# Turning the residual's blocks as fp32r in the last stage of a two-layer decoder trunk, with four blocks turned both ways

## The chip, the core and the metric

The kernel runs on one core of a Trainium2 chip. The metric is device time in microseconds, the median of several runs of the whole program; lower is better. A core has a matrix engine (PE, with its weight loads shown apart as PEld), a vector engine (DVE), a scalar engine (ACT), a general engine (POOL) and a queue that issues transfers (SP). Matrix products are written to PSUM, from which DVE and ACT read them; everything else lies in SBUF, and inputs and outputs in device memory.

## What is computed

Two pre-norm residual layers over a sequence of 1024 positions with 1024 features, and a last RMS norm. Layer 0 mixes with a gated linear recurrence, layer 1 with forgetting attention (16 heads of 64). The part that matters here is the end of layer 1 and the last norm:

```python
def fox_mixer(h, w_in, b_f, w_out):
    ...
    o = jnp.transpose(o, (1, 0, 2, 3, 4)).reshape(bsz, s, FOX_WIDTH).astype(h.dtype)
    y = o * jax.nn.silu(gate)
    return y @ w_out.astype(h.dtype)

def reference(x, ...):
    for i in range(DEPTH):
        h = rms_norm(x, norm_g[i])
        ...
            x = x + fox_mixer(h, fox_w_in[j], fox_b_f[j], fox_w_out[j])
    return rms_norm(x, final_g)
```

## The kernel before

The kernel keeps activations transposed: features on the 128 partitions, positions along the free axis, in two halves `c` of 512 positions. Products with 512 columns run in fp32r, a float32 that the matrix engine takes in one go at less precision; to keep precision, each operand is split into a high and a low part (`to_hi`, `to_lo`), and three products (high by high, high by low, low by high) are summed in PSUM. Blocks that are turned (`transpose`, or `matmul` with `is_transpose=True`) use the f32 identity `ident`, made at the start by POOL.

Layer 1 walks over the 16 heads. For each head and half, `maxima` computes scores and exponentials, and `weigh` turns these blocks (tile `pt`), splits them and multiplies them with the values (tile `O`). Between its steps `run` takes steps from a generator `fill`, which holds other work for PE; `side` holds more of it. In the last heads the fill is: the last projections, then `partial`, which adds six of the eight pairs of heads of the output projection to the residual and writes it back to the scratch tensor `x1d`, and then `turned`, the last stage. A scheduler of the framework, not the source alone, puts the instructions of each engine into their final order; within an engine the order is then fixed, and the engines wait for each other by semaphores.

`turned(c, q)` finishes a quarter of 256 positions. `residual` loads the residual so far from `x1d`, as eight blocks of 128 features by 256 positions. For each block `b` of 128 positions it goes over the features in parts (normally two of 512, in the very last block 512, 256 and 256). For each part it takes one PSUM buffer (tile `turn`), turns four (or two) residual blocks into it with the identity (line 921), and adds to it six products of the last two pairs of heads with the output weights. I call this one *group*: four turns and six products for 512 features. The stage has 17 groups: eight for c = 0 (two quarters, two blocks, two parts) and nine for c = 1.

A group is taken out of PSUM in two steps. ACT squares it with a running sum (`sq`, line 931), and DVE then multiplies it by the final norm's weights into `res` (line 933, or 939 for the last part of a block). DVE's step follows ACT's, and only then is the buffer free. The PSUM tag "g" has two buffers, as has "O"; groups use "g", apart from the first two groups of the second block of each quarter with c = 1, which use "O". The squares go to an SBUF scratch with the tag "xp", which has two buffers too.

For c = 0 the rows of the output wait for the whole half: `finish` (a `side` of the last run) takes one root for all four blocks (`root_mean`, lines 953 to 956, on the sums `ssq`), scales the four `res` (line 1058) and stores them (line 1059). For c = 1 each block has its own root, is scaled half by ACT (line 941) and half by DVE (line 942), and is stored (line 944). While c = 0 runs, the last head's work (`pt`, `O`) stands between and inside the groups on PE; the c = 1 part is PE groups alone.

Of the kernel before, what the change touches and what calls it, by code (L numbers as in the profile page):

```python
# [11 lines left out]
F32 = mybir.dt.float32  # L12
F32R = mybir.dt.float32r
BF16 = mybir.dt.bfloat16
AF = mybir.ActivationFunctionType
ALU = mybir.AluOpType

P = 128
SEQ = 1024
HALF = 512  # L20
# [18 lines left out]
def trunk(ctx: ExitStack, tc: tile.TileContext, xt, w0, wg, wo0, pc, gn, gf, w1, wv, wf, bf, wo1, out):  # L39
    nc = tc.nc  # L40

    def pool(name, bufs, **kw):
        return tc.tile_pool(name=name, bufs=bufs, **kw)

    const = ctx.enter_context(pool("const", 1))
# [3 lines left out]
    ps = ctx.enter_context(pool("ps", 2, space=PSUM))  # L49
# [3 lines left out]
    def matmul(*args, **kw):  # L53
        pe[0] = nc.tensor.matmul(*args, **kw)  # L54
        return pe[0]
# [5 lines left out]

    ident = const.tile([P, P], F32, name="ident")
    make_identity(nc, ident)
    onesf = const.tile([P, P], F32, name="onesf")
    nc.vector.memset(onesf, 1.0)
    epst = const.tile([P, 1], F32, name="epst")
# [116 lines left out]
    with ExitStack() as l0:  # L183
# [40 lines left out]
        xs = [[xpool.tile([P, HALF], F32, name=f"x{h}{k}") for k in range(KT)] for h in range(2)]  # L224
# [234 lines left out]
        for h, cs in enumerate(halves):  # L459
# [4 lines left out]
            for d0 in range(0, KT, 4):  # L464
                pts = []
                for db in range(d0, d0 + 4):
                    if db % 2 == 0:
                        two = ps.tile([P, 2, HALF], F32, tag="S", name="ops")
                    pts.append(two[:, db % 2])
                    mm3(pts[-1], wl[db][0], y[0], True, False)  # L470
                for db, o in enumerate(pts, d0):
                    mm3(o, wl[db][1], y[1], False, True)
                    x = xs[h][db]
# [18 lines left out]
    with ExitStack() as l1:  # L492
        tu = l1.enter_context(pool("tu", 1))
        at = l1.enter_context(pool("at", 2))
# [390 lines left out]
        def residual(c, q):  # L885

            cs = slice(q * 256, (q + 1) * 256)
            if c == q == 0:
                xs = [vpool.tile([P, 256], F32, tag=f"v{d}", name="x1", bufs=2) for d in range(KT)]
                for d, x in enumerate(xs):  # L890
                    nc.sync.dma_start(x, x1d[c, :, d, cs])
                return xs
            xs = [wpool.tile([P, 2, 256], F32, tag=("wl", "wh")[q], name="x1") for d in range(4)]
            for d, x in enumerate(xs):
                nc.sync.dma_start(x, x1d[c, :, 2 * d : 2 * d + 2, cs])
            return [x[:, i] for x in xs for i in range(2)]

        def turned(c, q):


            xs = left.pop((c, q), None) or residual(c, q)

            if c == 0:
                res = tu.tile([P, 2, SEQ], F32, tag=f"T{q}", name="res")
                res = [res[:, b] for b in range(2)]
            elif q == 0:
                res = [tu.tile([P, SEQ], F32, tag=t, name="res") for t in ("U", "U0")]
            else:
                res = [tu.tile([P, SEQ], F32, tag="U1", name="res"), at.tile([P, SEQ], F32, tag="p7", name="res", bufs=1)]
            for b in range(2):  # L910
                cs = slice(q * 256 + b * P, q * 256 + (b + 1) * P)

                parts = ((0, 4), (4, 2), (6, 2)) if c * q * b else ((0, 4), (4, 4))
                ss = ssq[c][:, 4 * q + 2 * b :][:, : len(parts)]
                for h, (d0, nd) in enumerate(parts):
                    hs = slice(d0 * P, (d0 + nd) * P)
                    pt = ps.tile([P, HALF], F32, tag="gO"[c * b] if h < 2 else "g", name="turn")[:, : nd * P]

                    for i in range(nd):
                        x = xs[d0 + i][:, b * P : (b + 1) * P]  # L920
                        matmul(pt[:, i * P : (i + 1) * P], x, ident, start=i == 0, stop=False, is_transpose=True)
                    for k in range(2):
                        yh, yl = (z[:, cs] for z in y1[c][6 + k])
                        wh, wl = (z[:, k::2][:, d0 % 4 : d0 % 4 + nd] for z in late_w[d0 // 4])
                        matmul(pt, yh, wh, start=False, stop=False)
                        matmul(pt, yl, wh, start=False, stop=False)
                        matmul(pt, yh, wl, start=False, stop=k == 1)
                        if k == 0:
                            yield
                    sq = at.tile([P, HALF], F32, tag="xp", name="sq1", bufs=2)[:, : nd * P]  # L930
                    nc.scalar.activation(sq, pt, AF.Square, accum_out=ss[:, min(h, ss.shape[1] - 1)].unsqueeze(1))
                    if c == 0 or h < len(parts) - 1:
                        nc.vector.tensor_tensor(res[b][:, hs], pt, grow[:, hs], ALU.mult)
                        if h == 1 and c == 1:
                            nc.vector.tensor_tensor(ss[:, 0:1], ss[:, 0:1], ss[:, 1:2], ALU.add)
                            ss = ss[:, 0::2]
                        yield
                if c == 1:
                    r = root_mean(ss, lambda: nc.vector.tensor_tensor(res[b][:, hs], pt, grow[:, hs], ALU.mult))
                    lo, hi = halves  # L940
                    nc.scalar.activation(res[b][:, lo], res[b][:, lo], AF.Copy, scale=r)
                    nc.vector.tensor_scalar(res[b][:, hi], res[b][:, hi], r, None, ALU.mult)
                    for hs in halves:
                        nc.sync.dma_start(out[4 + 2 * q + b, :, hs], res[b][:, hs])
                    yield
            if c == 0:
                first_half.extend(res)

        def root_mean(ss, between=lambda: None):

            ss = ss.rearrange("p (b h) -> p b h", h=2)
            r = ss[:, :, 0]
            nc.vector.tensor_tensor(r, r, ss[:, :, 1], ALU.add)
            between()
            nc.scalar.activation(r, r, AF.Sqrt, bias=epst, scale=1.0 / SEQ)
            nc.vector.reciprocal(r, r)
            return r
# [33 lines left out]
        for hd in range(HEADS):  # L991
            pair = hd // 2
            if hd % 2 == 0:
                if hd < 12:
                    fill = kq_units(pair + 1, ((1, (0, 1)), (0, (0,))))
                elif hd == 12:
                    pairs = ((0, 1), (2, 3), (4, 5), (6, 7))
                    todo = [(db, c) for two in pairs for c in range(2) for db in two]
                    splits = [split_loaded(c) for c in range(2)]
                    fill = chain(  # L1000
                        kq_units(7),
                        g_units(7, (0,)),
                        load_y(0),
                        first_out(),
                        beside(g_units(7, (1,)), 2, splits[0]),
                        load_y(1),
                        beside(beside(partial(todo), 0, splits[0]), 4, splits[1]),
                        turned(0, 0),
                        turned(0, 1),
                    )  # L1010
            elif pair < 6:
                fill = chain(kq_units(pair + 1, ((0, (1,)),)), late_q(hd + 1), g_units(pair + 1))
# [40 lines left out]
        def finish():  # L1053
# [3 lines left out]
            for i, o in enumerate(first_half):  # L1057
# [3 lines left out]
                yield  # L1061

        run("." * 20, fill=chain(turned(1, 0), turned(1, 1)), side=finish())


# [36 lines left out]
def build(arrays):  # L1102
    import concourse.bacc as bacc

    nc = bacc.Bacc("TRN2", target_bir_lowering=False, num_devices=1)
    args = [
        nc.dram_tensor(f"in_{k}", v.shape, mybir.dt.from_np(v.dtype), kind="ExternalInput").ap()
        for k, v in arrays.items()
    ]
    args.append(nc.dram_tensor("out_t", (KT, P, SEQ), F32, kind="ExternalOutput").ap())  # L1110
    with tile.TileContext(nc, schedule_with_timeline_sim=True) as tc:
        trunk(tc, *args)
    return nc
# [9 lines left out]
```

## Time and profile before

| what | value |
|---|---|
| median of 3 runs | 1123.81 us (1123.08 to 1123.89) |
| profiled execution, its span | 1127.7 us |
| PE busy, share of the span | 99% |
| PEld, DVE, ACT, POOL busy | 83%, 67%, 52%, 17% |
| groups of the last stage on PE | from about 1087.9 us to 1121.4 us |
| from the last product to the end of the span | 6.3 us |
| mean granted clock of PE | 0.998 |

The durations below come from one profiled execution; its span is longer than the time of the runs shown. A row of a timeline gives the start in us, the duration in us, the engine, the line and operation, what it writes and reads, the shape and how many instructions are merged into it, and in brackets how long the engine sat idle before and what released it. The start of a matmul is shown with its weight load (PEld) ahead of it; matmuls overlap, so the step of PE is read from start to start, not from the durations. A row of a group of instructions ends with busy time in us, mean duration in ns, and idle time before.

### The profile page before, as it was taken

The page shows a single profiled execution, that of the slowest core. Times are in us where ns is not written, and L with a number is a line of the kernel's source. Part 1 is how long each engine was busy: PE and PEld are TensorE (multiplying, and loading weights), DVE is VectorE, ACT ScalarE, POOL GpSimd, SP SyncE. Part 2 cuts the span into 40 slices and gives each one's busy share as a digit, 9 for nine tenths or more (in the row PEclk, how much of TensorE's full clock was granted, in tenths as well). Part 3 has the DMA queues.
Part 4 walks back from the last instruction along what each step waited for, and adds up shares of the span by engine and source line. Part 5 has one row for each costly group of instructions (what it writes and reads, how often), then busy time and mean ns, then how long its engine had stood idle before and what let it go on. Part 6 is the DMA issues. An engine that isn't in the chain of part 4 may idle for free.

```text
span 1127.7 us, 15774 instructions
## 1 busy us (share of the span) xinstructions
PE 1114.3 (99%) x5691; PEld 936.8 (83%) x5691; DVE 758.6 (67%) x1268; ACT 589.3 (52%) x1081; POOL 195.6 (17%) x155
## 2 busy tenths in 40 slices
PE   9999999999999999999999999999999999999997
PEld 7788888888888887988888988889888898888786
DVE  7888755776568789656676466664667646676545
ACT  8488345355453656365555355553555535644335
POOL 1322112221121201431021110212102110021220
PEclk9999999999999999999999999999999999999999
DMA  6111111111111114433425224242252422564345
GB/s 235 57 47 42 51 52 52 38 58 45 52 38 52 47 44 145 129 112 102 112 71 123 66 77 117 72 118 71 74 119 73 118 71 77 176 189 158 117 154 187
DMA packets 62902, 105.43 MB, mean 93 GB/s; under 512 B 9796, under 2 KB 24772, under 8 KB 62824
## 3 DMA queue, kind: packets, MB, share of 16 engines
q1 hardware_dynamic: 59704, 95.97, 28.9%
q0 software_dynamic: 3120, 8.46, 2.3%
q8 instruction: 45, 0.74, 0.3%
q14 instruction: 33, 0.27, 0.1%
HBM read 63.30 MB, written 15.93 MB: 70 GB/s over the span
## 4 chain that ended last, share of the span: by engine, by line
PE 92%; DMA 2%; DVE 2%; issue 1%; ACT 1%; SPq 1%; POOL 0%; DVEq 0%; POOLq 0%; ACTq 0%
PE gps L54 33%; PE ops L54 16%; PE ups L54 12%; PE vps L54 8%; PE S L54 6%; PE O L54 6%; PE pt L58 5%; PE gate L54 3%; PE turn L54 3%; DMA wf<-in_wo 1%; DMA x<-in_xt 1%; POOL wl L96 0%; PE rsrow L54 0%; DMA wf<-in_w 0%; DMA yhl<-y1d 0%
## 5 line engine op out<-in xcount | busy, mean ns | idle before, releaser
L54 PE MATMUL gps<-hh,wh 128*128 128x512 f32 x576 | 229.1, 398 | 0.6 <-DVE qkl L595 0.6
L54 PE MATMUL gps<-hh,wl 128*128 128x512 f32 x576 | 226.8, 394 | 0.0
L54 PE MATMUL gps<-hl,wh 128*128 128x512 f32 x576 | 226.7, 394 | 0.0
L85 ACT CAST wh<-wf 128x512 fp32r<-128x512 f32 (+2 forms) x156 | 94.2, 607 | 147.8 <-PE ops L54 55.3
L96 POOL TENSOR_TENSOR wl<-wf,wh 128x512 fp32r<-128x512 f32 (+1 forms) x60 | 101.0, 1689 | 389.8 <-ACT wh L85 362.5
L720 ACT ACTIVATE p<-S,m 128x128 f32<-128x128 f32 (+7 forms) x128 | 94.8, 741 | 137.9 <-DVE m L715 136.8
L96 DVE TENSOR_TENSOR pl<-pt,ph 128x512 fp32r<-128x512 f32 (+1 forms) x198 | 98.7, 540 | 88.1 <-ACT ph L85 87.6
L54 PEld LDWEIGHTS gps<-hl,wh 128*128 128x128 f32 x576 | 108.3, 188 | 24.7 <-issue 0.5
L54 PEld LDWEIGHTS gps<-hh,wh 128*128 128x128 f32 x576 | 108.6, 189 | 20.5 <-DVE qkl L595 0.8
L54 PEld LDWEIGHTS gps<-hh,wl 128*128 128x128 f32 x576 | 108.7, 189 | 20.1 <-POOL wl L96 0.6
L715 DVE CUSTOM_DVE_ANT_0 S<-S,mask 128x128 f32<-128x128 f32 (+7 forms) x128 | 97.3, 761 | 28.8 <-PE S L54 28.8
L85 ACT CAST ph<-pt 128x512 fp32r<-128x512 f32 (+1 forms) x198 | 83.6, 473 | 36.2 <-PE pt L58 28.9
L54 PE MATMUL S<-T,U 96*128 96x512 f32 (+7 forms) x384 | 91.9, 348 | 2.7 <-ACT p L720 2.7
L96 DVE TENSOR_TENSOR wl<-wf,wh 128x512 fp32r<-128x512 f32 x96 | 70.7, 741 | 28.3 <-ACT wh L85 27.4
L381 DVE TENSOR_TENSOR x<-x,ops 128x512 f32<-128x512 f32 x80 | 54.1, 683 | 48.0 <-PE ops L54 48.0
L54 PEld LDWEIGHTS S<-T,U 128*128 128x128 f32 (+1 forms) x384 | 68.6, 190 | 16.1 <-ACT p L720 3.5
L58 PE MATMUL pt<-ident,p 128*128 128x128 f32 x576 | 79.4, 273 | 0.8 <-DVE pl L96 0.5
L58 PEld LDWEIGHTS pt<-ident,p 128*128 128x128 f32 x576 | 67.2, 140 | 13.9 <-issue 2.9
L54 PE MATMUL ups<-hh,wh 128*128 128x512 f32 x192 | 76.1, 397 | 1.1 <-ACT hh L87 1.1
L54 PE MATMUL ups<-hl,wh 128*128 128x512 f32 x192 | 76.7, 399 | 0.2
L54 PE MATMUL ops<-yh,wh 128*128 128x512 f32 x192 | 76.0, 396 | 0.5 <-DVE x L474 0.5
L54 PE MATMUL ups<-hh,wl 128*128 128x512 f32 x192 | 76.2, 397 | 0.0
(183 smaller groups left out, 2247.8 us busy)
## 6 DMA issues: line engine op xcount, KB each, us to landing
wf<-in_w SPq DMA_DIRECT2D x100, 256.0 KB
wf<-in_wo SPq DMA_DIRECT2D x64, 128.0 KB
U<-qkh SPq DMA_DIRECT2D x64, 128.0 KB
T<-qkh SPq DMA_DIRECT2D x28, 256.0 KB
x<-in_xt SPq DMA_DIRECT2D x16, 256.0 KB
x1d<-x SPq DMA_DIRECT2D x16, 256.0 KB
wf<-in_wv SPq DMA_DIRECT2D x16, 256.0 KB
U<-qkl SPq DMA_DIRECT2D x32, 128.0 KB
```

The lines of the kernel that those rows point to most:

```text
L54: pe[0] = nc.tensor.matmul(*args, **kw)
L58: pe[0] = nc.tensor.transpose(*args)
L85: nc.scalar.copy(hi, src)
L96: return eng.tensor_tensor(lo, src, f32(hi), ALU.subtract)
L381: nc.vector.tensor_tensor(x, x, pt, ALU.add)
L715: nc.vector.tensor_tensor_reduce(S[:, :n], S[:, :n], mask[:, SEQ - n :], -1.0, -NEG, ALU.add, ALU.min, accum_out=m)
L720: seen[0] = nc.scalar.activation(p, S[:, :n], AF.Exp, bias=m, scale=-1.0, accum_out=sums[:, i : i + 1])
```

## The change

An fp32r copy of the identity is made once by ACT. The turns of the residual's blocks in the last stage take the residual and the identity as fp32r (the residual's bits as they are), and write PSUM as fp32r. For c = 0, after a quarter's groups, the first block of each `b` is turned twice into the two halves of a new PSUM tile `two` of the tag "g": once as fp32r, once as f32 as before. ACT copies the first result into `one` (scratch tag "xp"), DVE subtracts the second, and DVE adds 1e6 times the difference to the first 128 columns of `res`. So the output is changed wherever the two ways of turning differ. That makes four such pairs, and a step of the generator after each.

```diff
     ident = const.tile([P, P], F32, name="ident")
     make_identity(nc, ident)
+    identr = const.tile([P, P], F32R, name="identr")
+    nc.scalar.copy(identr, ident)
...
                     for i in range(nd):
                         x = xs[d0 + i][:, b * P : (b + 1) * P]
-                        matmul(pt[:, i * P : (i + 1) * P], x, ident, start=i == 0, stop=False, is_transpose=True)
+                        o = pt[:, i * P : (i + 1) * P].bitcast(F32R)
+                        matmul(o, x.bitcast(F32R), identr, start=i == 0, stop=False, is_transpose=True)
...
             if c == 0:
+                for b in range(2):
+                    x = xs[0][:, b * P : (b + 1) * P]
+                    two = ps.tile([P, HALF], F32, tag="g", name="two")
+                    matmul(two[:, :P].bitcast(F32R), x.bitcast(F32R), identr, start=True, stop=True, is_transpose=True)
+                    matmul(two[:, P : 2 * P], x, ident, start=True, stop=True, is_transpose=True)
+                    one = at.tile([P, HALF], F32, tag="xp", name="one", bufs=2)[:, :P]
+                    nc.scalar.copy(one, two[:, :P])
+                    nc.vector.tensor_tensor(one, one, two[:, P : 2 * P], ALU.subtract)
+                    nc.vector.scalar_tensor_tensor(res[b][:, :P], one, 1e6, res[b][:, :P], ALU.mult, ALU.add)
+                    yield
                 first_half.extend(res)
```

## The prediction

> **What bounds the kernel now.** I read the page first: busy shares, then the chain that ended last.
>
> ```profile
> span 1127.7 us, 15774 instructions
> ...
> PE 1114.3 (99%) x5691; PEld 936.8 (83%) x5691; DVE 758.6 (67%) x1268; ACT 589.3 (52%) x1081; POOL 195.6 (17%) x155
> ...
> PE 92%; DMA 2%; DVE 2%; issue 1%; ACT 1%; SPq 1%; POOL 0%; DVEq 0%; POOLq 0%; ACTq 0%
> ```
>
> TensorE is the bound, so what counts is PE time in the stage that changes, and every PE wait there. Second, the chain in order of time for that stage:
>
> ```profile
> 1097.38 1.84 PE turn L54 x10
> ...
> 1102.97 18.41 PE turn L54 x106
> 1121.38 0.02 issue
> ```
>
> From 1102.97 to 1121.38 the chain is PE alone. What follows (squares, root, scale, last store) takes 1127.7 - 1121.4 = 6.3 us and is not touched. Third, the timeline of this stage, PE beside what frees its PSUM buffers:
>
> ```profile
> 1102.40 0.28 PE L54 MATMUL O<-ph,v 128*128 128x256 f32 x1
> 1102.81 0.62 PE L54 MATMUL turn<-ident,x 128*128 128x128 f32 x4
> 1104.67 0.60 PE L54 MATMUL turn<-ident,x 128*128 128x128 f32 x4
> 1105.65 0.69 DVE L933 TENSOR_TENSOR res<-turn,grow 128x512 f32<-128x512 f32 x1 [1.12 <-ACT sq L931]
> 1106.26 0.40 PE L54 MATMUL turn<-wol,yhh 128*128 128x512 f32 x1
> 1106.39 0.47 PEld L54 LDWEIGHTS turn<-ident,x 128*128 128x128 f32 x4 [0.17 <-DVE res L933]
> 1106.50 0.60 PE L54 MATMUL turn<-ident,x 128*128 128x128 f32 x4
> 1106.76 0.60 ACT L931 ACTIVATE sq<-turn 128x512 f32<-128x512 f32 x1 [0.85 <-PE turn L54]
> 1107.48 0.69 DVE L933 TENSOR_TENSOR res<-turn,grow 128x512 f32<-128x512 f32 x1 [0.81 <-ACT sq L931]
> 1108.09 0.15 DVE L953 TENSOR_TENSOR ssq<-ssq 128x4 f32<-128x4 f32 x1
> 1108.22 0.49 PEld L54 LDWEIGHTS turn<-ident,x 128*128 128x128 f32 x4 [0.16 <-DVE res L933]
> 1108.34 0.60 PE L54 MATMUL turn<-ident,x 128*128 128x128 f32 x4
> ```
>
> I number the PSUM groups G1 to G17 in PE order; the starts shown are G7 (1102.81), G8, G9, G10 (1108.34). A full group takes 1106.50 - 1104.67 = 1.83 us. G8 ends at 1106.50, its buffer is free when DVE ends at 1108.17, and G10, the next user of that buffer, starts at 1108.34: **1.84 us from the end of a group to the reuse of its buffer**. The tag "g" has two buffers, and PE fills the other in 1.83 us. Eviction and PE are level; the weight loads already wait 0.16 to 0.17 us. Anything put between two groups that also takes a "g" buffer stops PE.
>
> **Cost of one turn.** What is PE's step, start to start, for a 128x128 turn, as f32 and as fp32r?
>
> ```profile
> 475.09 0.20 PEld L58 LDWEIGHTS fps<-ident,fz 128*16 128x16 f32 x2
> 475.31 0.19 PEld L54 LDWEIGHTS vps<-wh,hh 128*128 128x128 f32 x1
> ...
> 1089.23 0.19 PEld L54 LDWEIGHTS O<-pl,v 128*128 128x128 f32 x1
> 1089.35 0.19 PEld L54 LDWEIGHTS turn<-woh,yhh 128*128 128x128 f32 x1
> 1089.46 0.19 PEld L54 LDWEIGHTS turn<-woh,yhl 128*128 128x128 f32 x1
> ...
> 1120.85 0.28 PE L54 MATMUL turn<-woh,yhh 128*128 128x256 f32 x1
> 1120.97 0.28 PE L54 MATMUL turn<-woh,yhl 128*128 128x256 f32 x1
> ...
> L54 PEld LDWEIGHTS turn<-ident,x x64: 137/140/145, 1087.6 to 1120.3; 128*128 128x128 f32 x64
> L54 PEld LDWEIGHTS turn<-woh,yhh x34: 187/190/193, 1088.2 to 1120.7; 128*128 128x128 f32 x34
> ```
>
> A load begins when the matmul before it begins, so loads show the steps. f32: two fps turns with 16-column loads span 475.09 to 475.31, 0.11 us each; the load is short, so the 128 moved columns set the step. Six products in G8 take 6 x 0.23 of its 1.83 us, which leaves 0.45 / 4 = 0.11 again. For fp32r no turn is in the trace. Nearest from above: fp32r products with 128 moved columns and a load of their own, the two O products whose following loads start at 1089.23, 1089.35, 1089.46: 0.11 to 0.12. From below: fp32r moves 256 columns in 0.12 us, so half of that, 0.06, if no load binds. **I take 0.11**, since the O rows are the same type, width and pairing; every fp32r load in the quoted group takes 0.19 us, the f32 turn's only 0.14. So the 64 turns gain nothing; ends: 64 x -0.05 and 64 x +0.01 us.
>
> **The four pairs, in the built program's order.** Each adds an f32 and an fp32r turn (0.22 us) in a "g" buffer, an ACT copy, a DVE subtract (which frees the buffer) and a DVE multiply-add. Nearest rows for the 128x128 pieces:
>
> ```profile
> L96 DVE TENSOR_TENSOR pl<-pt,ph 128x128 fp32r<-128x128 f32 x33 | 9.3, 281 | 0.0
> L85 ACT CAST ph<-pt 128x128 fp32r<-128x128 f32 x33 | 9.1, 276 | 0.0
> L1058 DVE TENSOR_SCALAR res<-res,ssq 128x1024 f32<-128x1024 f32 x4 | 2.7, 749 | 0.0
> ...
> 1097.92 0.60 PE L54 MATMUL turn<-ident,x 128*128 128x128 f32 x4
> 1098.12 0.60 ACT L931 ACTIVATE sq<-turn 128x512 f32<-128x512 f32 x1 [0.49 <-PE turn L54]
> 1098.84 0.69 DVE L933 TENSOR_TENSOR res<-turn,grow 128x512 f32<-128x512 f32 x1 [0.42 <-ACT sq L931]
> ```
>
> First two pairs: they come after G4, which ends at 1097.92, where G5 starts now. The order is G4, pair 1, three pt turns, four O products, pair 2, all of G5, four O products, G6, G7. Pair 1 starts at once. After 0.22 + 0.33 + 0.48 us PE reaches pair 2 at 1098.95, and must wait for G4's buffer: DVE ends at 1099.53, plus the 0.16 us seen from a DVE end (1106.34) to the PE start (1106.50): 1099.69. G5 then needs pair 1's buffer: its subtract follows at once on DVE, 1099.53 + 0.28 + 0.16 = 1099.97. G5 1.83, O 0.41 (1102.40 to 1102.81), G6 1.83: G7 starts at 1104.04 instead of 1102.81. **+1.23 us.** The pairs' matmuls lie inside this. Behind the wait stand G5 and the last O products of the head; ACT's copy of these feeds the gated block that only G13 and later multiply, so it is not late.
>
> Second two pairs: G8, pair 3, pair 4, G9. With E the end of G8, pair 3 runs at once (G7's buffer is just free), and pair 4 needs G8's own buffer: E + 1.84. G9 needs pair 3's: DVE finishes G8's multiply, the ssq add (1108.09 + 0.15 is E + 1.74) and the subtract, E + 2.02; plus 0.16 is E + 2.18. Before, G9 started at E. **+2.18 us.** Queued behind this wait on PE are G9 to G17, all that is left.
>
> Late next: G10 needs pair 4's buffer. Its ACT copy stands behind G8's square, pair 3's copy, the 1.28 us table load and the root: about E + 3.1, subtract E + 3.4, start E + 3.56; G9 keeps PE until E + 4.01. Then DVE has three scales (0.69 apart), the fourth multiply-add and G9's multiply, done near E + 6.5; G13, the next in that buffer, starts at E + 9.5. The fourth multiply-add also holds the square scratch of G10, so that square waits to about E + 5.8, when G10 ends anyway. None reaches PE.
>
> The identity's copy at the start:
>
> ```profile
> 2.04 0.20 ACT L69 ACTIVATE root<-epst 128x1 f32<-128x1 f32 x1
> 3.32 0.62 ACT L85 CAST wh<-wf 128x512 fp32r<-128x512 f32 x1 [1.08 <-DMA wf<-in_w]
> ```
>
> It falls in 1.08 us in which ACT waits for the first weights: nothing; uncovered it would cost 0.28. No DMA is added; stores of the first half leave later with DVE's scales, yet over 10 us before the end.
>
> **Sum:** 1.23 + 2.18 = +3.4 us on the profiled execution (span 1127.7 to 1131.1). The page gives its span only, 3.9 us above the median of the runs, 1123.81; I carry the difference over: 1127.2, +0.30%.
>
> **Rivals.** *A, the fp32r turn has half the step, 0.06 us.* For it: an f32 turn is bound by moved columns (0.11 with a short load), and fp32r moves columns twice as fast (0.06 per 128). Against: the 0.19 us loads beside the 0.11 step of O. Each full group saves 0.2 us: G1 to G4 0.8; G5, G6 and G8 0.6 (G7's is lost, since G8 must wait for G6's buffer, 1.84 against 1.63 us); G9 to G17 1.6. So 3.4 - 3.0 = +0.4: 1124.2, not slower than before by what can be measured. It decides from about 0.09 us downward: 3.4 - 60 x 0.02 = 2.2 us. The Trainium skill (TensorEngine Tiling (Array Packing), Gotcha 2: Feature Incompatibilities) names a transpose mode for FP32 and FP32R input; if that brings the short 0.14 us load to fp32r too, the time would be A's. No fp32r turn is in this trace to agree or not.
>
> *B, the clock drops after the wait.*
>
> ```profile
> 1049.94 0.74 PE L54 MATMUL S<-T,U 128*128 128x512 f32 x2 [2.69 <-ACT p L720]
> ...
> 1050.68 4.35 PE ops L54 x12
> ...
> 1056.17 2.77 PE ops L54 x12
> ...
> 1040.00:1060.00 20.00, 17.31 (x79) 14.03 (x79) 11.56 (x22) 7.79 (x19) 4.11 (x5) 0.91 0.41 132
> ```
>
> After an idle stretch of 2.69 us the granted clock fell (0.91 over that slice) and twelve products took 4.35 instead of 2.77 us. The wait before pair 4 is 1.84 - 0.22 = 1.62 us, shorter, so I doubt it; its price is the same +1.6: 1128.8. The Trainium skill (TensorE: Matmul & The Clock Gate, Part 4) says transposes do not count as busy in the usual way; the idle stretch as the gate sees it would then run through pairs 3 and 4 and G9's turns, 2.6 us, and B's time would hold.
>
> *C, the waits are hidden and the step is halved:* 64 x -0.05 + 4 x 0.06 + 4 x 0.11 = -2.5: 1121.3, faster. The two-buffer rotation speaks against it.
>
> **How the numbers follow.** Forecast 0.50, A 0.32, B 0.12, C 0.06. Faster or slower counts from 0.2%, 2.2 us, about what a measurement of this kernel can tell from no change. Forecast and B are slower (0.62), A is the same (0.32), C faster (0.06). The range goes from just under A, 1124.0, to B, 1128.8, and leaves C out. The forecast's own is 1126.7 to 1127.9: the step at 0.12 adds 0.6, and the 0.28 us pieces may be shorter.
>
> **What would show it.** PE's waits before pair 2 (0.7 us), pair 4 (1.6) and G9 (0.2) on DVE res and the subtract; full groups in the c = 1 part at 1.83 us (at 1.63, A is right); loads of the fp32r turns at 0.19 (at 0.14, A gains); PEclk 1.0 to the end (else B). No PE wait at pairs 2 and 4 would make the sum wrong.

## The result and the profile after

| | before | after |
|---|---|---|
| median | 1123.81 us | 1126.38 us |
| ratio, 95% interval | | 1.0025, 1.0014 to 1.0036 |
| second series | 1124.82 us | 1126.35 us; 1.0018, 1.0005 to 1.0031 |
| span of the profiled execution | 1127.7 us | 1124.8 us |

The first series has seven runs of each kernel, the second 23 and 12. The changed kernel is slower by 2.6 us in the first series and 1.5 us in the second. One run of the changed kernel in the first series took 2232.87 us at a granted clock of 1.0; the ratio leaves it out, and no trace shows why it was long. The two spans say the opposite, and can't be compared: the profiled execution of before held the 2.69 us wait near 1049 us that the prediction quoted, and that of after did not. So I compare the last stage alone. The page of the changed kernel begins:

```profile
span 1124.8 us, 15807 instructions
...
PE 1112.4 (99%) x5699; PEld 935.2 (83%) x5699; DVE 757.0 (67%) x1276; ACT 590.5 (52%) x1086; POOL 195.2 (17%) x155
```

PE still bounds it. The chain of waits gives a measure of the last stage, from the start of its first `turn` row to the end of its last. The first such row of before (start, us, what) was:

```profile
1088.02 1.14 PE turn L54 x7
```

With the end quoted in the prediction, 1121.38, the stage before took 33.36 us. The same chain of the changed kernel:

```profile
1083.25 1.05 PE turn L54 x7
...
1092.99 0.17 PE two L54 x2
1093.16 0.34 PE pt L58 x3
...
1093.75 0.70 DVE res L936
1094.45 0.14 issue
1094.59 0.39 PE two L54 x2
1094.97 1.75 PE turn L54 x10
1096.72 0.41 PE O L54 x4
1097.13 5.33 PE turn L54 x30
...
1103.27 0.70 DVE res L936
1103.97 0.04 issue
1104.01 0.41 PE two L54 x2
1104.42 14.23 PE turn L54 x86
```

The stage takes 1118.65 - 1083.25 = 35.40 us, **+2.04 us**. Before, the chain had no engine but PE from 1102.97 on; now it leaves PE twice for DVE's `res`, just ahead of pair 2 and of pair 4, as forecast. Between the stops PE is faster: a row of ten pieces takes 1.75 us, where it took 1.84. The timeline shows the second stop (brackets: idle time before, and what ended it):

```profile
1102.28 0.26 PE L54 MATMUL two<-identr,x 128*128 128x128 f32 x1
1103.27 0.69 DVE L936 TENSOR_TENSOR res<-turn,grow 128x512 f32<-128x512 f32 x1 [1.06 <-ACT sq L934]
1103.94 0.28 DVE L957 TENSOR_TENSOR one<-one,two 128x128 f32<-128x128 f32 x1
1104.01 0.28 PE L54 MATMUL two<-identr,x 128*128 128x128 f32 x1 [1.33 <-DVE res L936]
1104.28 0.53 PE L54 MATMUL turn<-identr,x 128*128 128x128 f32 x4
1106.11 0.46 PE L54 MATMUL turn<-identr,x 128*128 128x128 f32 x4
1107.86 0.46 PE L54 MATMUL turn<-identr,x 128*128 128x128 f32 x4
1109.61 0.46 PE L54 MATMUL turn<-identr,x 128*128 128x128 f32 x4
```

Pair 4 starts 1.73 us after the end of G8 (1102.28), G9 2.00 us after it. The starts of G10 to G12 are 1.75 us apart: a full group is some 0.08 us shorter than the 1.83 of before. The granted clock in this stage, by windows (start:end and length, busy us and instructions of PE, PEld, DVE, ACT, POOL, the clock, DMA share, GB/s):

```profile
1092.00:1098.00 6.00, 5.39 (x38) 4.69 (x37) 3.47 (x10) 3.16 (x11) 0.00 (x0) 1.00 0.01 3
1098.00:1104.00 6.00, 4.67 (x27) 3.49 (x25) 3.04 (x8) 3.11 (x9) 0.74 (x1) 1.00 0.43 131
1104.00:1111.00 7.00, 6.99 (x41) 5.84 (x42) 6.11 (x16) 3.99 (x11) 0.00 (x0) 1.00 0.70 267
```

It stays at 1.00 through and behind both stops.

My theory from here on, S ("stops"): the time is two stops of PE for a "g" buffer, some 3.2 us together, less a saving of about 0.02 us on each fp32r turn. The rivals: the turns save nothing and the stops are smaller; or one stop brings about the other; or the placement of the pairs' buffer costs nothing and something else stops PE.

### The profile page after: what moved, and what is told of

Read it like the earlier page. It is cut to its first block, busy times and chain, and to the rows that moved or that the text cites. A ratio compares the mean times of both kernels' runs of the same rounds, so it can differ in the third digit from the quotient of the medians.

```text
span 1124.8 us, 15807 instructions
## 1 busy us (share of the span) xinstructions
PE 1112.4 (99%) x5699; PEld 935.2 (83%) x5699; DVE 757.0 (67%) x1276; ACT 590.5 (52%) x1086; POOL 195.2 (17%) x155
## 4 chain that ended last, share of the span: by engine, by line
PE 94%; DVE 2%; ACT 1%; DMA 1%; issue 1%; POOL 0%; SPq 0%; POOLq 0%; ACTq 0%; DVEq 0%
PE gps L54 33%; PE ops L54 17%; PE ups L54 12%; PE vps L54 8%; PE O L54 6%; PE S L54 6%; PE pt L58 6%; PE gate L54 3%; PE turn L54 3%; PE rsrow L54 0%; DMA x<-in_xt 0%; DMA yhl<-y1d 0%; POOL wl L98 0%; PE sscol L54 0%; ACT yhh L87 0%
## 5 line engine op out<-in xcount | busy, mean ns | idle before, releaser
L98 DVE TENSOR_TENSOR wl<-wf,wh 128x512 fp32r<-128x512 f32 x96 | 67.6, 708 | 27.0 <-ACT wh L87 26.1
```

The source lines that it names most:

```text
L98: return eng.tensor_tensor(lo, src, f32(hi), ALU.subtract)
```

## The experiments

The stage's length, taken from the chain as above, is the measure; the medians stand beside it. What the traces show of the medians' scatter stands at the end of this part.

### The turns alone

The loop over `b` that makes the pairs is left out:

```diff
             if c == 0:
-                for b in range(2):
-                    x = xs[0][:, b * P : (b + 1) * P]
...
                 first_half.extend(res)
```

> The fp32r turns alone, without the four pairs. Theory S (the fp32r turn's step is 0.09 us against 0.11, and the pairs cost waits on PSUM buffers): full groups of the c = 1 part at 1.76 us as in the changed kernel, against 1.83 before; 15 full groups save 0.075 us and two short ones half of it, so about -1.2 us against before. Rival N (the turns gain nothing, groups were shortened by something in the new order): groups at 1.83 and the time of before, 0 +- 0.3 us. Rival H (the step halves once no pair stands beside it): groups at 1.63, -3 us.

1122.89 us, ratio 0.9992 (0.9983 to 1.0001). From its chain:

```profile
1085.04 1.05 PE turn L54 x7
...
1099.51 17.73 PE turn L54 x106
```

Stage 32.20 us, -1.16 against before. The last 106 pieces take 17.73 instead of 18.41 us, with no stop. So the turns do save time: 1.16 / 64 = 0.018 us each.

The same kernel a second time:

> The fp32r turns without any pair a second time, since its first interval (0.9983 to 1.0001) touched 1. If every full group is 0.07 us shorter and nothing else changes: stage -1.1 us, time 1122.7 us, ratio 0.999, with a PE that never stops between G1 and the last product. The rival: the 0.07 us are lost in the eviction's pace (1.84 us from the end of a group to the reuse of its buffer), groups 1.83, ratio 1.000.

1123.07 us, ratio 0.9988 (0.9974 to 1.0001). From its chain:

```profile
1087.07 1.05 PE turn L54 x7
...
1101.51 17.74 PE turn L54 x106
```

Stage 32.18 us: the saving repeats within 0.02 us. Both medians lie below that of the kernel before (1124.43 and 1124.27 us in the two series, so by 1.5 and 1.2 us), and no other kernel here does better; but both intervals end at 1.0001. That it beats the kernel before is shown for the stage, and likely but not shown for the whole run.

### The pairs alone

The groups' turns stay f32; the pairs are as in the changed kernel:

```diff
-                        o = pt[:, i * P : (i + 1) * P].bitcast(F32R)
-                        matmul(o, x.bitcast(F32R), identr, start=i == 0, stop=False, is_transpose=True)
+                        matmul(pt[:, i * P : (i + 1) * P], x, ident, start=i == 0, stop=False, is_transpose=True)
```

> The four pairs alone; the 64 turns of the groups stay f32. Theory S: group starts as in the changed kernel but 1.83 us a group; G5 about 1.95 us after the end of G4, G9 about 2.0 us after the end of G8; +1.2 and +2.0 us, so about +3.2 us against before, which is the forecast's sum less the overlap of the subtract with the multiply ahead of it. Rival N: the same as the changed kernel, +2.6 us.

1127.08 us, ratio 1.0032 (1.0018 to 1.0046). From its chain:

```profile
1082.63 1.14 PE turn L54 x7
...
1104.42 14.77 PE turn L54 x86
```

Stage 36.56 us, +3.20. The 86 pieces behind pair 4 take 14.77 us with f32 turns, 14.23 with fp32r. The change is the sum of its parts: -1.16 + 3.20 = +2.04, which is what its own stage shows.

### The pairs in another PSUM tag

The pairs take their PSUM buffer from tag "S" in place of "g". That tag holds the scores, which are done by then, and the `pt` blocks, which end ahead of G6:

```diff
-                    two = ps.tile([P, HALF], F32, tag="g", name="two")
+                    two = ps.tile([P, SEQ], F32, tag="S", name="two")[:, :HALF]
```

> The changed kernel with the tile of the pairs in the PSUM tag of the score tiles (two buffers of two banks, idle by then) and not in the groups' tag; same matmuls, copies, subtracts and multiply-adds. Theory S: the second stop (1.6 us before pair 4 and 0.2 before G9) goes, since pairs 3 and 4 find free buffers; the first one stays about as it is, since pair 2 now needs pair 1's buffer, whose subtract stands behind G4's multiply on DVE. So -2.0 us plus 0.35 for the two pairs' matmuls that were inside the stop: about +0.9 us against before. Rival W (the pairs' own work on ACT and DVE delays the end, whichever buffer they use): no better than the changed kernel, +2.6 us.

1126.79 us, ratio 1.0021 (1.0009 to 1.0032). By its median this contradicts S, which expected 0.9 us over before and not 2.4. The chain says otherwise:

```profile
1082.70 1.05 PE turn L54 x7
...
1093.88 0.20 DVE one L957
...
1094.13 0.42 PE two L54 x2
...
1098.50 0.35 PE two L54 x4
1098.85 17.68 PE turn L54 x106
```

Stage 33.84 us, +0.48 against before and 1.56 less than the changed kernel; the last two pairs take only 0.35 us: the scheduler put their four matmuls in one piece behind G6, and no stop follows. The first stop is left: `pt` still uses the tag there, and pair 2 waits for DVE's subtract of pair 1, which itself stands behind G4's `res`. Times and trace disagreed, so I ran it again beside the changed kernel.

> The kernel with the pairs in tag S a second time, beside the changed kernel on the same chip, since its first times lay in two groups (four near 1124.5, eight from 1126.3 to 1129.3). If those are the scatter that profiles show ahead of the last stage (a PE wait of 2 to 3 us near 1048 for ACT's p), its stage is again 33.8 us from the first turn to the last product, its lowest times 1.6 us below those of the changed kernel, and its median, over the same scatter, 0.5 to 2 us below. The rival: the placement costs the time elsewhere (S buffers held by the pairs stop the next S), then the median is no lower than the changed kernel's and the profile shows a wait of PE on S behind the pairs.

> The changed kernel itself a second time, for its scatter. Both theories: stage 35.4 us from the first turn to the last product, lowest time 1125.4, median 1126.4 to 1127.5.

1124.53 us (ratio 1.0000, 0.9988 to 1.0012), the changed kernel 1126.35 us; lowest times 1123.45 and 1125.23 us. From the chain of the second run with tag "S":

```profile
1086.85 1.05 PE turn L54 x7
...
1102.68 0.35 PE two L54 x4
1103.03 17.67 PE turn L54 x106
```

Stage 33.85 us again (the changed kernel, again, 35.41). So 1.56 us of the stage, and 1.8 us of the median in this series, hang on which PSUM tag the pairs take, with every instruction of them still there. The order hangs on it too: with the other tag the scheduler puts pairs 3 and 4 behind G6 and not behind G8, and no run parts the tag from the place. The stage is the same in both runs of this kernel, so the 2.3 us between their medians are put down to scatter; no long execution of the first run has a trace. The rival with a cost elsewhere falls.

### Two pairs at a time

The loop runs for one quarter only; shown is the first, the other has `q == 1`:

```diff
-                for b in range(2):
+                for b in range(2 * (q == 0)):
```

> The fp32r turns and pairs 1 and 2 alone; pairs 3 and 4 are left out. If each stop is priced by itself, as the changed kernel's trace reads (its stretch with pairs 1 and 2 +1.05 us, with pairs 3 and 4 +2.00, its full groups 0.07 shorter each, -1.0 in all), the stage from its first turn to its last product takes +0.05 us against before and 2.0 us less than in the changed kernel; one PE wait on DVE's res before pair 2, none before G9, which begins right behind G8. The rival: one stop is enough to put PE and the eviction out of step, so that the second stretch waits too (another 0.5 us or more between G8 and G10). Time by the first: 1124 us, within 0.2% of before.

1125.50 us, ratio 1.0012 (0.9998 to 1.0027). From its chain:

```profile
1082.07 1.05 PE turn L54 x7
...
1095.95 19.49 PE turn L54 x116
```

Stage 33.37 us. The 116 pieces from the second O products on run without a stop; in the changed kernel the same pieces with pairs 3 and 4 take 1118.65 - 1097.13 = 21.52 us. So the second stop costs 2.03 us, and the first, against the turns alone, 33.37 - 32.20 = 1.17.

> The fp32r turns and pairs 3 and 4 alone; pairs 1 and 2 are left out. If each stop is priced by itself, the stage takes +1.0 us against before (+2.00 for the stop behind G8, -1.0 for the groups), with PE waiting 1.3 us or more before pair 4 on DVE's res; 1.05 us less than the changed kernel. The rival: without the first stop the eviction runs closer behind PE and the second is longer than 2.2 us. Time by the first: 1124.8 us.

1125.13 us, ratio 1.0006 (0.9991 to 1.0021). From its chain:

```profile
1082.75 1.05 PE turn L54 x7
...
1097.22 3.57 PE turn L54 x20
...
1102.76 14.21 PE turn L54 x86
```

Stage 34.22 us. Up to the row of 20 it takes 14.47 us, as the turns alone do to their row of 106 (1099.51 - 1085.04 = 14.47); from there 19.75 us against 17.73, which is 2.02 for the second stop. Either stop costs the same without the other: both rivals that tie them together fall.

### The step of a turn by itself

The turns alone, and behind the last group five bursts of eight matmuls, 128 moved columns each, into an otherwise idle buffer, released at once: f32 turns (ba), fp32r turns (bb), both again with weight loads of 16 columns (bc, bd), and fp32r products with a load of their own (be). The kernel ran once, in 1123.19 us; only its trace counts here.

```diff
+        def t_f32r(o, i):
+            matmul(o.bitcast(F32R), identr, identr, start=True, stop=True, is_transpose=True)
...
+        def n_f32r(o, i):
+            matmul(o[:16].bitcast(F32R), identr[:, i * 16 : (i + 1) * 16], identr, start=True, stop=True, is_transpose=True)
```

> The kernel of the first experiment with five bursts of eight 128-column matmuls behind the last group, back to back on PE, whose results nothing reads: f32 turns with 128-column loads, fp32r turns with 128-column loads, f32 turns with 16-column loads, fp32r turns with 16-column loads, fp32r products with 128-column loads. If the fp32r turn is bound by its load, its step falls from 0.09 us to 0.06 with 16-column loads while the f32 turn stays at 0.11; if it is bound by the moved columns at one and a half times the rate of a product, it stays at 0.08 to 0.09 with either load. fp32r products with their own 128-column loads: 0.11 to 0.12, bound by the 0.19 us load.

The chain of this kernel:

```profile
1115.11 0.87 PE ba L54 x8
1115.98 0.64 PE bb L54 x8
1116.62 0.87 PE bc L54 x8
1117.49 0.48 PE bd L54 x8
1117.97 0.89 PE be L54 x8
```

The row of a burst ends where the next begins. Divided by eight: an f32 turn takes 0.109 us with either load; an fp32r turn 0.080 with a load of 128 columns, 0.060 with one of 16; an fp32r product with a load of its own 0.111. The timeline's rows of loads for two of the bursts (start, time from the first load's start to the last one's end):

```profile
1115.71 0.77 PEld L54 LDWEIGHTS bb<-identr 128*128 128x128 f32 x8
...
1117.22 0.56 PEld L54 LDWEIGHTS bd<-identr 128*16 128x16 f32 x8
```

With a load of 0.14 us, seven steps of bb take 0.77 - 0.14 = 0.63 us, 0.090 each; with 0.09, seven of bd take 0.47, 0.067 each. The chain and the loads don't place the ends of a burst alike (for bc the loads give (0.78 - 0.09) / 7 = 0.10, the chain 0.109), so the step of bb lies between 0.08 and 0.09; the groups give 0.109 - 0.018 = 0.091. The fp32r turn's step falls by a quarter with the narrow load, the f32 turn's by a tenth at most. That fits an fp32r turn bound by its load and an f32 turn bound by its 128 moved columns. But a turn with a load of 16 columns also writes only 16 partitions of PSUM, and no run parts the two. Not tried: the blocks of exponentials (`pt`) turned as fp32r, 576 turns in the whole kernel, where they too might gain.

### Why the medians scatter

Eleven profiles were taken, of eight kernels. In four of them PE stops once near 1048 us, in the attention part, ahead of a score product; the other seven have no such stop. One is the execution of before in the prediction. The timeline of the turns alone has it in this row:

```profile
1048.50 0.73 PE L54 MATMUL S<-T,U 128*128 128x512 f32 x2 [2.31 <-ACT p L722]
```

Their second run has it at 1049.04 us, with an idle time of 2.10 us; the second run with tag "S" at 1048.83, with 2.50. In each, the chain runs back through DVE and ACT to a transfer of the output weights (`wf` from `in_wo`). ACT's copy of these weights begins at 1044.7 to 1046.2 us in the four, at 1042.1 to 1043.8 in the seven. This delay is only part of the stop. Behind the copy DVE subtracts it from the weights (`wl`), and in the four that begins while POOL multiplies `sg`. The timeline of the turns alone:

```profile
1044.56 2.36 POOL L749 TENSOR_TENSOR sg<-sg,recb 64x1024 f32<-64x1024 f32 x1 [1.30 <-DMA recb<-recd]
1045.12 2.08 DVE L98 TENSOR_TENSOR wl<-wf,wh 128x256 fp32r<-128x256 f32 x1 [1.55 <-ACT wh L87]
```

The same subtract in the timeline of the changed kernel, where POOL's product begins only at 1047.54:

```profile
1044.33 0.42 DVE L98 TENSOR_TENSOR wl<-wf,wh 128x256 fp32r<-128x256 f32 x1
```

In the four the subtract takes 2.06 to 2.09 us and ends 0.28 to 0.29 us behind POOL's product; in the seven it is done before that product begins and takes 0.41 to 0.42. So some 1.65 us of the stop is DVE's. The changed kernel has another such pair: a `wl` subtract of this size starts at 1005.38, inside a product of POOL that ends at 1006.70, and takes 1.60 us, again to 0.28 us behind it. That POOL's product holds the subtract up is likely; no run moved one of them to show it.

The last stage then begins at 1085.0 to 1088.0 us, where the other seven have 1082.0 to 1083.3: between 2 and 6 us that arise ahead of the stage. That the same stop makes the long ones among the executions without a trace is likely, not shown.

## Why the prediction was right, and where it was off

**Direction and size.** Forecast were 1127.2 us and +3.4; measured 1126.38 and +2.6 in the runs, +2.04 in the stage. Slower for the reason given: two stops of PE for a "g" buffer. The size was over-forecast: the forecast's own range began at 1126.7 us, and both medians, 1126.38 and 1126.35, lie below it. The prediction took 2.2 us, 0.2%, as the least that counts as slower. The first series is above that; the second (+1.5) and the stage (+2.04, 0.18%) are just below. So the mechanism was right, but that the first result came out as slower by this measure, and not as the same, owes something to luck.

**The term that was mis-sized: "I take 0.11" and "So the 64 turns gain nothing".** The fp32r turn's step is 0.091 us, and 64 x 0.018 us give 1.16 us back. The nearest row, the O product with a load of its own, was a true measure of that kind (be: 0.111), but the wrong neighbour. The view of one tile of the changed kernel (minimum, median, maximum in ns) has the reason:

```profile
L54 PEld LDWEIGHTS turn<-identr,x x64: 137/140/144, 1082.9 to 1117.6; 128*128 128x128 f32 x64
...
L54 PEld LDWEIGHTS turn<-woh,yhh x34: 186/187/193, 1083.3 to 1118.0; 128*128 128x128 f32 x34
```

The load of an fp32r turn takes 140 ns, like that of the f32 turn, not the product's 187. I had expected 0.19 from the loads beside it, so the point that should have moved the estimate was whether turning, not the type, sets the load. Full groups then took 1.75 us, between the 1.83 of the forecast and the 1.63 of rival A.

**Rival A (half the step, 0.06 us)** was half right. Moved columns go at nearly twice the rate (bd 0.060, bc 0.109), and the load is the short one, 140 ns, so the condition that A's paragraph set was met. The Trainium skill (TensorEngine Tiling (Array Packing), Gotcha 2: Feature Incompatibilities) lists a transpose mode for FP32 and FP32R input only. It says nothing of its load, so the 140 ns are this trace's own. The condition was met, and still the time was not A's: with a load of 128 columns the step stays at 0.08 to 0.09 us. The step came out at the edge that A's paragraph named, "about 0.09 us downward", where its sum gave +2.2; the stage gave +2.04.

**The first stop, +1.23.** Measured 1.17. The wait before pair 2 was forecast at 0.7 us; the timeline of the changed kernel has 0.61. Pair 2 came 0.14 us behind the end of DVE's `res`, as the chain's "issue" row shows, close to the 0.16 assumed.

**The second stop, +2.18.** Measured 2.02 to 2.03. The wait before pair 4 was forecast at 1.6 us and measured at 1.33. Pair 4 came 1.73 us after the end of G8, not 1.84, since PE started 0.05 us behind the end of `res` (1103.27 + 0.69 to 1104.01) and not 0.16. G9 came after 2.00, without a wait of its own where 0.2 was forecast: DVE's subtract began as `res` ended, so the ssq add that I had put between them delayed nothing. This is 0.15 us of the 3.4.

**Late next: nothing.** G10 started 1.83 us after G9, with no wait of PE in the timeline, and from there the groups follow at 1.75 to 1.77 up to the last full one; neither the scales nor the fourth multiply-add reached PE. The identity's copy cost nothing either, as forecast: it took 0.28 us on ACT, which still waited 1.10 us for the first weights.

**Rival B (the clock drops after the wait)** did not happen: the granted clock is 1.00 in all the windows above. The Trainium skill (TensorE: Matmul & The Clock Gate, Part 4: PE-mode transpose) says that transposes don't count as busy in the same way. No run here agrees: neither pairs 3 and 4 with G9's turns nor the bursts of turns (a window over them reads 1.00) lowered the clock, though the four bursts of turns last only 2.86 us together. B was not far, though. The window around the 2.10 us wait near 1049, in the second run of the turns alone, reads a clock of 0.91:

```profile
1040.00:1060.00 20.00, 17.91 (x82) 14.50 (x81) 12.44 (x25) 7.33 (x18) 5.05 (x6) 0.91 0.47 138
```

In the same window the waits of 2.50 and 2.69 us gave 0.91 as well, that of 2.31 us 1.00, so the length alone doesn't decide it; the 1.33 us wait ahead of pair 4 left the clock at 1.00.

**Rival C (waits hidden)** is excluded: the stops stand in the chain of every kernel that has the pairs in "g".

Taken together, 3.41 forecast - 1.16 (turns) - 0.06 (first stop) - 0.15 (second) = 2.04, the stage's measured difference.

## What to carry to other kernels

Where PE and the eviction of PSUM run level with two buffers, even a tiny piece between two groups can cost a whole eviction if it takes one of those buffers: the last two pairs, 0.4 us of matmuls, cost 2.0 us in the groups' tag and 0.35 us in an idle one, where the scheduler also placed them earlier. The first two, with other work of PE between them, cost 1.17. To price an operation that the trace doesn't show, look for a row that shares what bounds it, not for one of the same type: the f32 turn's short load told more of the fp32r turn than an fp32r product did. When the effect is a tenth of a per cent and the runs scatter by more, compare one stage of the traces and let the parts add up.

## What was not expected of the hardware

An fp32r turn of a 128x128 block gains only 0.018 us over the f32 turn's 0.109, though with a load of 16 columns it takes 0.060. And near 1045 us, in four of eleven profiles, one transfer of weights lands late enough for DVE's subtract to fall beside a product of POOL; the subtract then takes 2.1 us in place of 0.42, and the last stage begins 2 to 6 us later, as much as the change costs or more.
